# A GeGLU down projection in fp32: the order of seven-product blocks and plain K-tiles, and the step in which block sums of weights are made

## The chip, the core and the metric

The kernel runs on one core of one Trainium2 chip. A core has a matrix engine (TensorE, PE in the profile; its weight loads are listed apart as PEld), a vector engine (VectorE, DVE), a scalar engine (ScalarE, ACT), a general engine (GpSimd, POOL) and a queue engine (SyncE, SP), each with an instruction stream of its own that runs in order. They meet through semaphores. SBUF holds operands in 128 partitions, PSUM takes matmul results in eight banks of 128x512 fp32, and DMA engines move data between HBM and SBUF. The metric is the device time of one execution in microseconds (us); lower is better.

## The reference

One decoder layer on x of 256 tokens by 2048 channels, all in float32. A first half mixes tokens (eight attention heads beside sixteen state-space heads) and adds the result to x. The second half is the feed-forward part, in which the change lies:

```
h = rms_norm(x, ln_ffn_pre)
u = causal_depthwise_conv(h @ w_ffn_up, ffn_conv_w, ffn_conv_b)      # 2048 -> 2 * 5632, three taps
gate, up = jnp.split(u, [FFN_HIDDEN], axis=-1)
f = (jax.nn.gelu(gate, approximate=True) * up) @ w_ffn_down         # 5632 -> 2048
x = x + rms_norm(f, ln_ffn_post)
```

## The kernel before, in words

**Products.** A float32 product is made of three matmuls. Each operand is split into a rounded part (hi, type fp32r) and the rest (lo): hi times hi, hi times lo and lo times hi are added up in PSUM. Activations are split once. Weights are split as they arrive: a unit of weights is 128x1024 fp32 (512 KB). SP issues its load into a tile `raw` (four buffers), ACT casts it to `whi`, DVE subtracts to get `wlo` (lines 80 to 82). `whi` and `wlo` have four buffers and, from the feed-forward part on, three more, so units are prepared seven ahead of the one that PE works on. `take` hands PE the next prepared unit, `tick`, called after each unit, prepares one more. A cast into a buffer waits until PE has finished with the unit that was there.

**The feed-forward part** works in two halves of 22 hidden K-tiles (128 channels each). In each half PE first makes the up projection (`cols_tile`, lines 245 and 246) for gate and up of each K-tile; ACT and DVE do the convolution, the GELU and the product (`conv_ffn`, `gated`) and split the result. Then comes the down projection, once for output columns 0 to 1023 and once for 1024 to 2047: two calls of `down_pair` per half, four in all.

**Inside `down_pair`.** The first eight K-tiles of the half form four blocks of two K-tiles (QUADS = 4). A block is a 2x2 by 2x2 matrix product (token halves by K-tiles, K-tiles by 512 columns), made with seven products in place of eight (`product`, lines 1084 to 1086, three matmuls of 512 columns each). The seven need sums of weight blocks. So a block takes four steps of the weight stream, in `quad_step`: "col" (a loaded unit, split whole), "next" (a loaded unit, of which one half is split), "two" (a tile `ts` of two sums, split whole) and "more" (a tile `ts` of two further sums, split whole). The sums are DVE additions of 128x512 (line 137, two for each `ts`), written in the source ahead of the cast (line 138) and the subtraction (line 139) of the same step. PE does two, one, two and two products in the four steps. The other 14 K-tiles (PLAIN) go two to a unit, seven units for the first 512 columns and seven for the second, with 12 matmuls to a unit (`rows_part`, lines 309 to 311).

In each call all four blocks come first, then the 14 plain units. Four of the products' sums stand in PSUM banks `pa` (p1, p6, p7, q5), the other three go into three of the four banks `ph`, into which the plain units then add too. After the last block ACT and DVE add the four `pa` banks up in SBUF (lines 1113 to 1127); when a `ph` bank is complete, `fdone` adds it (line 1014). In the very last call the last five plain units are held and worked off token half by token half, so that the first half's norm and store run beside the second's matmuls.

**Order.** Each engine runs its stream in order. The framework that builds the streams lists instructions by their place in the source and by when it estimates that their operands are ready, so neighbours can change places: lines 1084 and 309 of a later unit stand among lines 1085 and 1086 of an earlier one in places.

**The norm weight.** Before the two down calls of the second half a POOL-issued DMA brings the post-norm weight, spread over 128 partitions (1024 KB, line 1162), into a tile `late` that reuses the memory of the up projection's input; ACT then multiplies it by -0.5 (line 1163).

Of the kernel before, what the change touches and what calls it, by code (L numbers as in the profile page):

```python
# [9 lines left out]
F32 = mybir.dt.float32  # L10
# [17 lines left out]
FF = 5632  # L28
NF = FF // P
HALF = NF // 2  # L30
QUADS = 4
PLAIN = HALF - 2 * QUADS
EPS = 1e-6
NEG = -1e30
# [22 lines left out]
def f32(ap):  # L57
    return ap.bitcast(F32)


class Weights:
# [54 lines left out]
    def quad_step(self, i, kind, src=None):  # L116

        nc, q = self.nc, self.quad  # L120
        hi, lo = (self.place(i, n, SPLB, F32R)[:, :UE] for n in ("whi", "wlo"))
        self.ready.append((hi, lo))
        n = UE
        if src is not None:
            q[kind] = raw = self.place(i, "raw", RAWB, F32)
            nc.sync.dma_start(out=raw, in_=src)
            n = UE if kind == "col" else 512
        else:
            q[kind] = raw = self.sums.tile([P, UE], F32, name="ts", tag="ts", bufs=2)
            a, b = raw[:, :512], raw[:, 512:]  # L130
            if kind == "two":
                pairs = (a, q["col"][:, 512:], q["next"][:, 512:]), (b, q["next"][:, :512],
                                                                     q["next"][:, 512:])
            else:
                pairs = (a, q["two"][:, :512], q["next"][:, :512]), (b, a, q["col"][:, :512])
            for dst, x, y in pairs:
                nc.vector.tensor_tensor(dst, x, y, op=ALU.add)  # L137
        nc.scalar.copy(hi[:, :n], raw[:, :n])  # L138
        return lambda: nc.vector.tensor_tensor(lo[:, :n], raw[:, :n], f32(hi[:, :n]),  # L139
                                               op=ALU.subtract)  # L140

# [13 lines left out]
def decoder_layer(ctx, tc, x, xT, win, wdt, wout, wup, wdown, relb, vec, cols, mconv, fconv,  # L155
# [17 lines left out]
    def psum(name):  # L173
        return msc.tile([P, 512], F32, name=name, tag="m")
# [123 lines left out]
    def col_psum():  # L298
        return acc.tile([P, 512], F32, name="pa", tag="a")
# [43 lines left out]
    def units(w, a, n, shift=0):  # L343
        return [(w[i], shift) for i in range(a, a + n)]

    def down_units(half):

        found, at = [], half * 44
        for _ in range(2):
            for j in range(QUADS):  # L350
                found += [("col", wdown[at]), ("next", wdown[at + 1]), ("two",), ("more",)]
                at += 2
            found += units(wdown, at, PLAIN)
            at += PLAIN
# [722 lines left out]
        nc.scalar.copy(hi, src)  # L1077
        nc.vector.tensor_tensor(lo, src, f32(hi), op=ALU.subtract)

    def product(ps, j, block, w, h, more=False):  # L1080

        a, b = (gx[j][:, c, :][:, tok(block)] for c in range(2))
        s = chunk(h)
        nc.tensor.matmul(ps, a, w[0][:, s], start=(j == 0), stop=False)
        nc.tensor.matmul(ps, a, w[1][:, s], start=False, stop=False)
        end[0] = nc.tensor.matmul(ps, b, w[0][:, s], start=False,
                                  stop=(j == QUADS - 1 and not more)).ins

    def down_pair(half, c):

        p1, p6, p7, q5 = (col_psum() for _ in range(4))
        pss = [[psum("ph"), psum("ph")] for _ in range(2)]
        for j in range(QUADS):
            w = ws.take()
            product(p1, j, 0, w, 1)
            product(pss[0][0], j, 1, w, 0, True)
            tick()
            w = ws.take()  # L1100
            product(pss[1][0], j, 6, w, 0, True)
            tick()
            w = ws.take()
            product(q5, j, 3, w, 0)
            product(p7, j, 5, w, 1)
            tick()
            w = ws.take()
            product(p6, j, 4, w, 0)
            product(pss[0][1], j, 2, w, 1, True)
            tick()  # L1110
        f = [[fa[:, t, chunk(c + n)] for t in range(NT)] for n in range(2)]
        tt = nc.vector.tensor_tensor
        if half == 0:
            nc.scalar.copy(f[0][0], p1)
            tt(f[1][0], p6, f[0][0], op=ALU.add)
# [3 lines left out]
        else:  # L1119
            nc.scalar.copy(e[0], p1)  # L1120
            tt(f[0][0], e[0], f[0][0], op=ALU.add)
            tt(e[0], p6, e[0], op=ALU.add)
            tt(e[1], p7, e[0], op=ALU.add)
            tt(f[0][1], e[1], f[0][1], op=ALU.add)
            for n in range(2):
                tt(f[1][n], q5, f[1][n], op=ALU.add)
                tt(f[1][n], f[1][n], e[n], op=ALU.subtract)
        n = PLAIN // 2
        for h in range(2):
            last = half == 1 and c == 2 and h == 1  # L1130
            for i in range(n - HOLD * last):
                w = ws.take()
                for t in range(NT):
                    rows_part(pss[h][t], w, gT, 2 * i, t, i == 0 and h * t == 1, i == n - 1)
                tick()
            if not last:
                for t in range(NT):
                    fdone(half, c + h)(t, pss[h][t])
        if half == 1 and c == 2:
            fearly.extend(early_sum(ss[2][t][:, :3]) for t in range(NT))  # L1140
            tail = [ws.take() for _ in range(HOLD)]
            for t in range(NT):
                for i in range(HOLD):
                    rows_part(pss[1][t], tail[i], gT, 2 * (n - HOLD + i), t, False, i == HOLD - 1)
                fdone(1, 3)(t, pss[1][t])

    defer(5, lambda: along_tokens(rb2, [sums[:, t:t + 1] for t in range(NT)]))
    for half in range(2):
        for i in range(half * HALF, (half + 1) * HALF):
            ps = held_up[2 * i:2 * i + 2]  # L1150
            for _ in range(2 - len(ps)):
                ps.append(col_psum())
                cols_tile(ps[-1], h2)
            us = [summed(p) for p in ps]
            if i < 2:
                defer(5 - 2 * i, gated, i, *us)
            else:
                gated(i, *us)
        if half == 1:
            late = pers.tile([P, D + 1024], F32, name="late", tag="h", bufs=1)  # L1160
            wpo, e = late[:, :D], [late[:, D:D + 512], late[:, D + 512:]]
            aux(out=wpo, in_=row_bcast(V_FFNPOST, D))
            nc.scalar.mul(wpo, wpo, -0.5)
        for c in (0, 2):
            down_pair(half, c)

# [104 lines left out]
```

## Time and profile before

| | |
|---|---|
| median of 3 runs | 1108.06 us (1106.46 to 1108.73) |
| the profiled execution | 1109.13 us, its span 1107.2 us |
| PE busy | 1095.1 us, 99% of the span, 5840 matmuls |
| DVE busy | 876.2 us, 79% |
| ACT busy | 617.0 us, 56% |
| DMA | 217.59 MB, mean 197 GB/s |
| mean granted TensorE clock | 0.996 of full speed |

A row of the timeline reads: start in us, duration in us, engine, line of the kernel, operation, what is written and what is read, shapes, and in brackets the idle time of the engine just before with what ended it. Matmul durations overlap (a matmul of 512 columns is listed with 0.39 us, but the next starts 0.23 us later), so time on PE is read from the distance between starts. The listing of waits gives total us, times, and the longest in us. A very few matmul records are missing.

### The profile page before, as it was taken

Reading aid. Unit: us, or ns where it says so; the run is one execution under the profiler, and the core shown is the slowest. Engines: PE = TensorE matmul, PEld = TensorE weight load, DVE = VectorE, ACT = ScalarE, POOL = GpSimd, SP = SyncE. Lnnn points to the kernel's source line nnn. Section 1 sums busy time; section 2 is a strip of 40 time slices with the busy share of each in tenths; the row PEclk is TensorE's granted clock in tenths of the full one; section 3 lists DMA queues with packets and bytes.
Section 4 is the critical chain, followed back from the end, with each engine's and each line's share of the span. In section 5 each row is a group of like instructions: output and inputs, shape, how many; then the busy total and the mean of one; then the engine's idle time right before and its main releaser. Section 6 shows DMA issues by size and latency. Waiting matters only on the chain.

```text
span 1107.2 us, 15885 instructions
## 1 busy us (share of the span) xinstructions
PE 1095.1 (99%) x5840; PEld 937.2 (85%) x5840; DVE 876.2 (79%) x1418; ACT 617.0 (56%) x938; POOL 16.2 (1%) x26
## 2 busy tenths in 40 slices
PE   9999999999999999999999999999999999999997
PEld 7888888888888988888888788888888888877886
DVE  6699976776566799888788988758788878898885
ACT  6666545545454486555555655545555555565452
POOL 0010000000000000000000000000000000000000
PEclk9999999999999999999999999999999999999999
DMA  8868545555587266666565284866556656538362
GB/s 283 303 192 269 183 152 162 180 173 170 206 305 248 86 226 226 194 190 193 189 190 188 107 274 130 286 192 191 191 190 190 191 190 190 179 127 278 132 235 78
DMA packets 61358, 217.59 MB, mean 197 GB/s; under 512 B 7200, under 2 KB 8624, under 8 KB 60384
## 3 DMA queue, kind: packets, MB, share of 16 engines
q1 hardware_dynamic: 59328, 207.64, 57.8%
q0 software_dynamic: 1664, 8.59, 2.1%
q8 instruction: 46, 0.75, 0.3%
q10 hardware_dynamic: 288, 0.35, 0.1%
q14 instruction: 32, 0.26, 0.1%
HBM read 214.44 MB, written 2.11 MB: 196 GB/s over the span
## 4 chain that ended last, share of the span: by engine, by line
PE 93%; DVE 3%; DMA 1%; ACT 1%; issue 1%; SPq 0%; POOLq 0%; ACTq 0%; DVEq 0%
PE pa L245 36%; PE pa L246 18%; PE pa L309 5%; PE pa L310 5%; PE pa L311 5%; PE ph L309 5%; PE ph L310 5%; PE ph L311 5%; DVE wlo L139 1%; PE pab L245 1%; DVE ts L137 1%; PE pa L254 1%; PE py L645 1%; PE pab L246 1%; DMA late<-in_vec_dram 1%
## 5 line engine op out<-in xcount | busy, mean ns | idle before, releaser
L81 ACT CAST whi<-raw 128x1024 fp32r<-128x1024 f32 (+2 forms) x357 | 369.7, 1039 | 337.1 <-PE pa L245 176.8
L82 DVE TENSOR_TENSOR wlo<-raw,whi 128x1024 fp32r<-128x1024 f32 (+2 forms) x357 | 429.4, 1208 | 154.1 <-ACT whi L81 147.1
L245 PE MATMUL pa<-h,whi 128*128 128x512 f32 x1360 | 471.7, 394 | 0.0
L246 PE MATMUL pa<-h,wlo 128*128 128x256 f32 x1360 | 379.1, 279 | 0.0
L245 PEld LDWEIGHTS pa<-h,whi 128*128 128x128 f32 x1360 | 255.5, 188 | 57.5
L246 PEld LDWEIGHTS pa<-h,wlo 128*128 128x128 f32 x1360 | 255.3, 188 | 0.0
L245 PE MATMUL pa<-hT,whi 128*128 128x512 f32 x384 | 137.0, 398 | 0.0
L246 PE MATMUL pa<-hT,wlo 128*128 128x256 f32 x384 | 107.1, 281 | 0.0
L309 PE MATMUL ph<-whi,gT 128*128 128x512 f32 x224 | 87.7, 392 | 0.2 <-ACT whi L81 0.2
L311 PE MATMUL ph<-whi,gT 128*128 128x512 f32 x224 | 87.4, 390 | 0.0
L310 PE MATMUL ph<-wlo,gT 128*128 128x512 f32 x224 | 87.4, 390 | 0.0
L245 PEld LDWEIGHTS pa<-hT,whi 128*128 128x128 f32 x384 | 72.5, 189 | 15.5 <-issue 0.2
L1005 DVE SCALAR_TENSOR_TENSOR cfc<-cfu,fcv,cfc 128x255 f32<-128x255 f32 (+1 forms) x176 | 83.1, 477 | 1.6 <-ACT cfc L1003 0.4
L246 PEld LDWEIGHTS pa<-hT,wlo 128*128 128x128 f32 x384 | 72.3, 189 | 0.4 <-issue 0.2
L1003 ACT ACTIVATE cfc<-cfu,fcv 128x256 f32<-128x256 f32 x88 | 52.2, 598 | 1.1 <-DVE cfu L1002 1.1
L138 ACT CAST whi<-ts 128x1024 fp32r<-128x1024 f32 x32 | 33.5, 1048 | 33.8 <-DVE ts L137 14.4
L309 PE MATMUL pa<-whi,hT 128*128 128x512 f32 x128 | 51.1, 400 | 0.0
L309 PEld LDWEIGHTS ph<-whi,gT 128*128 128x128 f32 x224 | 42.3, 189 | 9.5 <-ACT whi L81 0.7
L309 PE MATMUL pa<-whi,mT 128*128 128x512 f32 x128 | 50.3, 393 | 0.0
L311 PE MATMUL pa<-whi,hT 128*128 128x512 f32 x128 | 50.1, 392 | 0.0
L310 PE MATMUL pa<-wlo,hT 128*128 128x512 f32 x128 | 50.0, 390 | 0.0
L310 PE MATMUL pa<-wlo,mT 128*128 128x512 f32 x128 | 50.0, 390 | 0.0
(257 smaller groups left out, 1340.2 us busy)
## 6 DMA issues: line engine op xcount, KB each, us to landing
raw<-in_wup_dram SPq DMA_DIRECT2D x176, 512.0 KB, 3.6
raw<-in_wdown_dram SPq DMA_DIRECT2D x88, 512.0 KB, 4.3
raw<-in_win_dram SPq DMA_DIRECT2D x85, 512.0 KB, 3.6
raw<-in_wout_dram SPq DMA_DIRECT2D x32, 512.0 KB, 4.1
xsq<-in_x_dram SPq DMA_DIRECT2D x2, 1024.0 KB, 9.2
rows<-acd POOLq DMA_DIRECT2D x4, 512.0 KB, 6.7
xt<-in_x_dram POOLq DMA_DIRECT2D x2, 1024.0 KB, 6.8
xr<-in_xT_dram SPq DMA_DIRECT2D x6, 256.0 KB, 6.8
```

The lines of the kernel that those rows point to most:

```text
L81: nc.scalar.copy(hi[:, s], raw[:, s])
L82: return lambda: nc.vector.tensor_tensor(lo[:, s], raw[:, s], f32(hi[:, s]), op=ALU.subtract)
L137: nc.vector.tensor_tensor(dst, x, y, op=ALU.add)
L138: nc.scalar.copy(hi[:, :n], raw[:, :n])
L139: return lambda: nc.vector.tensor_tensor(lo[:, :n], raw[:, :n], f32(hi[:, :n]), op=ALU.subtract)
L245: nc.tensor.matmul(ps, w[0][:, s], both, start=(k == 0), stop=False)
L246: end[0] = nc.tensor.matmul(ps[:, c], w[1][:, s], hi, start=False, stop=(k == KT - 1)).ins
L309: nc.tensor.matmul(ps, a, w[0][:, s], start=(first and j == 0), stop=False)
L310: nc.tensor.matmul(ps, a, w[1][:, s], start=False, stop=False)
L311: end[0] = nc.tensor.matmul(ps, b, w[0][:, s], start=False, stop=(last and j == 1)).ins
L1003: nc.scalar.activation(c, u, AF.Identity, scale=wv[:, 2:3], bias=wv[:, 3:4])
L1005: nc.vector.scalar_tensor_tensor(c[:, sh:], u[:, :S - sh], wv[:, 2 - sh:3 - sh], c[:, sh:], op0=ALU.mult, op1=ALU.add)
```

## The change

Four edits. First, the order inside `down_pair` is now a string, ORDER, read once per call: Q is a block with its four steps, 0 and 1 are plain units for the first and the second 512 columns. There are still four blocks and seven plain units for each 512 columns, and the last five entries are the ones held in the very last call. The list of weight units and the host's array follow the same string, in `down_units` and in the host code.

Second, the steps of a block are now "same" (split whole), "other" (one half split), "two" and "more". The sums of "two" are made in step "other", with one addition of 128x1024 whose second operand repeats a half unit twice; the sums of "more" are made in step "two", with two additions of 128x512. The two loaded units hold other pairs of blocks than before, so that this works.

Third, the multiplication of the post-norm weight by -0.5 is issued not ahead of the second half's down calls but in the first of them, behind its fourth block.

Fourth, the additions of the four `pa` banks move into `quad_sums`, which is called behind the fourth block, so ahead of the plain units that follow it. `fdone` for the first 512 columns is called behind the seventh unit 0.

```
+ORDER = "0Q01Q001Q0Q0011111"
+QUADS = ORDER.count("Q")
...
+        else:
+            raw = q[kind]
+        if kind == "other":
+            n = 512
         nc.scalar.copy(hi[:, :n], raw[:, :n])
+        if kind == "other":
+            q["two"] = to = self.sums.tile([P, UE], F32, name="ts", tag="ts", bufs=2)
+            two = (ap.rearrange("p (b c) -> p b c", b=2) for ap in (to, q["same"]))
+            add(*two, raw[:, None, 512:].to_broadcast([P, 2, 512]), op=ALU.add)
+        elif kind == "two":
+            q["more"] = to = self.sums.tile([P, UE], F32, name="ts", tag="ts", bufs=2)
+            add(to[:, :512], raw[:, :512], q["same"][:, 512:], op=ALU.add)
+            add(to[:, 512:], to[:, :512], q["other"][:, :512], op=ALU.add)
         return lambda: nc.vector.tensor_tensor(lo[:, :n], raw[:, :n], f32(hi[:, :n]),
                                                op=ALU.subtract)
...
+        for what in ORDER[:-HOLD] if last else ORDER:
+            if what == "Q":
+                for items in (((p1, 0, 0), (pss[1][0], 6, 1)), ((pss[0][0], 1, 0),),
+                              ((q5, 3, 0), (p7, 5, 1)), ((p6, 4, 0), (pss[0][1], 2, 1))):
+                    multiply(items, ws.take())
+                    tick()
+            else:
+                w, h, i = ws.take(), int(what), done[what]
                 for t in range(NT):
+                    rows_part(pss[h][t], w, gT, 2 * i, t, first(pss[h][t]), i == n - 1)
                 tick()
+            done[what] += 1
+            if what == "Q" and done[what] == QUADS:
+                if half == 1 and c == 0:
+                    nc.scalar.mul(wpo, wpo, -0.5)
+                quad_sums(half, c, *once)
+            elif what != "Q" and done[what] == n:
                 for t in range(NT):
                     fdone(half, c + h)(t, pss[h][t])
...
             aux(out=wpo, in_=row_bcast(V_FFNPOST, D))
-            nc.scalar.mul(wpo, wpo, -0.5)
```

More of the change, by code (lines that the diff above doesn't have):

```diff
@@ L116, in quad_step @@
     def quad_step(self, i, kind, src=None):
-        nc, q = self.nc, self.quad
+        nc, q, add = self.nc, self.quad, self.nc.vector.tensor_tensor
         hi, lo = (self.place(i, n, SPLB, F32R)[:, :UE] for n in ("whi", "wlo"))
@@ L348, in down_units @@
         found, at = [], half * 44
-        for _ in range(2):
-            for j in range(QUADS):
-                found += [("col", wdown[at]), ("next", wdown[at + 1]), ("two",), ("more",)]
+        for what in 2 * ORDER:
+            if what == "Q":
+                found += [("same", wdown[at]), ("other", wdown[at + 1]), ("two",), ("more",)]
                 at += 2
-            found += units(wdown, at, PLAIN)
-            at += PLAIN
+            else:
+                found += units(wdown, at, 1)
+                at += 1
         return found
@@ L1078, in quad_operands, with product, quad_sums @@
         nc.vector.tensor_tensor(lo, src, f32(hi), op=ALU.subtract)
-    def product(ps, j, block, w, h, more=False):
+    def product(ps, j, block, w, h, first, last):
         a, b = (gx[j][:, c, :][:, tok(block)] for c in range(2))
         s = chunk(h)
-        nc.tensor.matmul(ps, a, w[0][:, s], start=(j == 0), stop=False)
+        nc.tensor.matmul(ps, a, w[0][:, s], start=first, stop=False)
         nc.tensor.matmul(ps, a, w[1][:, s], start=False, stop=False)
[L1086 to L1110, printed above, removed]
+        end[0] = nc.tensor.matmul(ps, b, w[0][:, s], start=False, stop=last).ins
+    def quad_sums(half, c, p1, p6, p7, q5):
         f = [[fa[:, t, chunk(c + n)] for t in range(NT)] for n in range(2)]
@@ L1118, in down_pair @@
             tt(f[1][0], q5, f[1][0], op=ALU.subtract)
[L1119 to L1132, printed above, removed]
+            return
@@ new lines, in quad_sums, with down_pair, first, multiply @@
+        nc.scalar.copy(e[0], p1)
+        tt(f[0][0], e[0], f[0][0], op=ALU.add)
+        tt(e[0], p6, e[0], op=ALU.add)
+        tt(e[1], p7, e[0], op=ALU.add)
+        tt(f[0][1], e[1], f[0][1], op=ALU.add)
+        for n in range(2):
+            tt(f[1][n], q5, f[1][n], op=ALU.add)
+            tt(f[1][n], f[1][n], e[n], op=ALU.subtract)
+    def down_pair(half, c):
+        once = [col_psum() for _ in range(4)]
+        p1, p6, p7, q5 = once
+        pss = [[psum("ph"), psum("ph")] for _ in range(2)]
+        begun, done, n = set(), {"Q": 0, "0": 0, "1": 0}, PLAIN // 2
+        def first(ps):
+            new = id(ps) not in begun
+            begun.add(id(ps))
+            return new
+        def multiply(items, w):
+            for ps, block, h in items:
+                product(ps, done["Q"], block, w, h, first(ps),
+                        done["Q"] == QUADS - 1 and any(ps is z for z in once))
+        last = half == 1 and c == 2
+        for what in ORDER[:-HOLD] if last else ORDER:
+            if what == "Q":
+                for items in (((p1, 0, 0), (pss[1][0], 6, 1)), ((pss[0][0], 1, 0),),
[4 more added lines that the diff above has]
+                w, h, i = ws.take(), int(what), done[what]
@@ L1137, in down_pair @@
                 for t in range(NT):
                     fdone(half, c + h)(t, pss[h][t])
-        if half == 1 and c == 2:
+        if last:
             fearly.extend(early_sum(ss[2][t][:, :3]) for t in range(NT))
```

31 lines of the change are left out of this document (13 added, 18 removed).

## The prediction

> **What bounds the kernel now.** I began with the page's first part and its chain of waits.
>
> ```profile
> PE 1095.1 (99%) x5840; PEld 937.2 (85%) x5840; DVE 876.2 (79%) x1418; ACT 617.0 (56%) x938; POOL 16.2 (1%) x26
> PE 93%; DVE 3%; DMA 1%; ACT 1%; issue 1%; SPq 0%; POOLq 0%; ACTq 0%; DVEq 0%
> ```
>
> PE carries the time. The change takes no matmul away: four blocks of 21 matmuls and 14 plain units of 12 make 4 x 21 + 14 x 12 = 252 per down call, before and after. So it can only win what PE loses inside the four down calls. Next come the starts of PE's instructions at the calls' borders, from the timeline.
>
> ```profile
> 616.36 0.39 PE L1084 MATMUL pa<-whi,gx 128*128 128x512 f32 x1
> ...
> 637.33 0.39 PE L309 MATMUL ph<-whi,gT 128*128 128x512 f32 x1
> ...
> 675.41 0.39 PE L1084 MATMUL pa<-whi,gx 128*128 128x512 f32 x1
> ...
> 732.95 0.40 PE L245 MATMUL pa<-h,whi 128*128 128x512 f32 x1
> ...
> 977.01 0.39 PE L1084 MATMUL pa<-whi,gx 128*128 128x512 f32 x1
> ...
> 1040.22 0.39 PE L1084 MATMUL pa<-whi,gx 128*128 128x512 f32 x1
> ...
> 1097.60 1.25 PE L1029 MATMUL pa<-xt,cst 128*128 128x256 f32 x6
> ```
>
> The 168 plain matmuls of the first call run from 637.33 to 675.41: 0.2267 us each, so a call without a pause is 252 x 0.2267 = 57.12 us. The four calls take 59.05 (616.36 to 675.41), 57.54, 63.21 and 57.38 us. PE loses 1.93 + 0.42 + 6.09 + 0.26 = 8.70 us there: that is all there is to win. The rest after 1097.60 is the last norm and store, which keeps its five held units. The pauses themselves, first call and third:
>
> ```profile
> 633.60 0.73 PE L1084 MATMUL pa<-whi,gx 128*128 128x512 f32 x2 [0.51 <-ACT whi L138]
> 634.92 0.50 PE L1084 MATMUL pa<-whi,gx 128*128 128x512 f32 x1 [0.59 <-ACT whi L138]
> ...
> 989.61 0.50 PE L1085 MATMUL pa<-wlo,gx 128*128 128x512 f32 x1 [0.62 <-DVE wlo L139]
> ...
> 998.45 0.50 PE L1084 MATMUL pa<-whi,gx 128*128 128x512 f32 x1 [2.27 <-ACT whi L138]
> ...
> 999.73 0.74 PE L1085 MATMUL pa<-wlo,gx 128*128 128x512 f32 x1
> 1000.27 0.63 PE L1086 MATMUL pa<-whi,gx 128*128 128x512 f32 x1
> ...
> 1003.23 0.40 PE L310 MATMUL ph<-wlo,gT 128*128 128x512 f32 x1
> ```
>
> All lie near the end of the four blocks, and PE waits for the split of block weights. Behind the 2.27 us pause eight starts take 1003.23 - 999.73 = 3.50 us where 1.81 were due: PE ran at about half clock, which makes 1.69 of the 6.09 us.
>
> Why the splits are late is read on DVE, inside the first call:
>
> ```profile
> 629.38 1.82 DVE L139 TENSOR_TENSOR wlo<-raw,whi 128x1024 fp32r<-128x1024 f32 x2
> 631.12 1.29 DVE L137 TENSOR_TENSOR ts<-raw 128x512 f32<-128x512 f32 x2
> 632.32 1.41 DVE L137 TENSOR_TENSOR ts<-ts,raw 128x512 f32<-128x512 f32 x2
> 633.65 2.48 DVE L139 TENSOR_TENSOR wlo<-ts,whi 128x1024 fp32r<-128x1024 f32 x2
> 636.04 4.62 DVE L82 TENSOR_TENSOR wlo<-raw,whi 128x1024 fp32r<-128x1024 f32 x4
> 640.59 0.68 DVE L1115 TENSOR_TENSOR fa<-pa,fa 128x512 f32<-128x512 f32 x1
> ```
>
> One block costs DVE 636.04 - 629.38 = 6.66 us without a gap, and PE only 21 x 0.2267 = 4.76. A plain unit costs DVE 4.55 / 4 = 1.14 us and PE 12 x 0.2267 = 2.72. Four blocks in a row put DVE 4 x 1.90 = 7.6 us behind; the prepared lead pays for most of it, and PE stands for the rest. Over a whole call DVE needs 4 x 6.66 + 14 x 1.14 = 42.6 us of 57.12: the average fits, the order doesn't.
>
> The third call has an extra cause, seen on ACT, in the chain of waits and in SP's waits:
>
> ```profile
> 983.94 1.92 ACT L1163 ACTIVATE late<-late 128x2048 f32<-128x2048 f32 x1 [1.81 <-DMA late<-in_vec_dram]
> 985.76 0.39 ACT L232 CAST gT<-cfc 128x256 fp32r<-128x256 f32 x1
> ```
> ```profile
> 989.47 0.70 DVE ts L137
> 990.18 4.12 DMA raw<-in_wdown_dram
> 994.40 1.06 ACT whi L81
> ```
> ```profile
> SPq L80 <- DVE ts L137: 17.2, 4, 10.2
> ```
>
> ACT stands 1.81 us for the norm weight's DMA and then works 1.92 us on it, with casts and the last K-tile's products queued behind. The block sums come late, they keep the `raw` buffers, the next load starts only at 990.18 and lands 4.12 us later, and PE stands at 996. The third call loses 6.09 - 1.93 = 4.16 us more than the first, whose blocks stand in the same order.
>
> **The interleaved order.** I count PE time from a call's start. The order gives 0 at 0, first block 2.72, two units, second block at 2.72 + 4.76 + 5.44 = 12.92, three units, third block 25.8, one unit, fourth block 33.3, done by 38.1. How much is prepared at the start is shown by ACT:
>
> ```profile
> 613.67 0.62 ACT L138 CAST whi<-raw 128x512 fp32r<-128x512 f32 x1 [1.45 <-PE pa L245]
> ...
> 616.44 1.05 ACT L138 CAST whi<-ts 128x1024 fp32r<-128x1024 f32 x1 [1.84 <-PE pa L245]
> ```
>
> These are steps six and seven of the weight stream (second block's "next" and "two"): at 616.4 seven steps are there or in work. In the old order seven steps hold 4.76 us and most of a second block, some 8 us of PE. In the new they are 0, block, 0, 1: 12.9 us. In that time DVE owes the second block, 6.66, and the rest of the last K-tile's convolution, eight instructions between and with these two:
>
> ```profile
> 618.66 0.42 DVE L263 TENSOR_TENSOR cfu<-pa,cfu 128x256 f32<-128x256 f32 x1
> ...
> 624.72 0.41 DVE L233 TENSOR_TENSOR gT<-cfc,gT 128x256 fp32r<-128x256 f32 x1
> ```
>
> At some 0.45 each that is 3.6 us, together 10.3 of the 12.9. A cast waits until PE is done seven steps back. The tightest is then the fourth block's "two": free when PE finishes the third block's "same", at 27.2, needed at 33.3 + 3 x 0.68 = 35.4; 8 us for a cast of 1.05 and a subtraction of 1.22. The third block falls due 12.9 us behind the second and the fourth 7.5 behind the third, against 6.66 + 3 x 1.14 = 10.1 and 7.8 of DVE time; the 0.3 come out of that lead. So the DVE pauses go: up to 1.93 + 0.42 + 0.26, and 1.93 of the third call's. What is late next is nothing on PE's inputs; its own 57.12 us is.
>
> A rule of the Trainium skill bears on the half-clock stretch, in "TensorE: Matmul & The Clock Gate", Part 1: the clock falls back only after an idle window of about 3.4 us. Here it fell with a longest idle row of 2.27 us. By this rule of the Trainium skill the 1.69 us would not belong to this pause and would stay, and the sum would be 1102.1. The trace has them right behind the pause, so I count them with it.
>
> **The sums one step ahead.** Line 137 runs ahead of earlier splits already:
>
> ```profile
> 958.84 0.69 DVE L137 TENSOR_TENSOR ts<-raw 128x512 f32<-128x512 f32 x1 [0.17 <-DMA raw<-in_wdown_dram]
> 959.45 1.22 DVE L82 TENSOR_TENSOR wlo<-raw,whi 128x1024 fp32r<-128x1024 f32 x1
> ```
>
> So I give this edit zero of its own, beyond letting `raw` go a step sooner. It turns two additions of 0.60 (starts of line 137) into one of 1024 columns with a repeated operand, which no row shows; the nearest is 1.14 for 1024 columns. Between 0.06 us gained and, if the repeat doubled it, 1.1 lost per block, it lies beside PE: DVE has 57.12 - 42.6 = 14.5 us a call, less 4.2 for seven additions of `pa` and 4.8 for `fdone` (eight of 0.60), 5.5 left; four times 1.1 still fits. I take 0.06, off the path. The new addition needs its loaded unit, and DVE's queue (subtractions, evacuations) stands behind it; PE's seven-step lead covers that (priced below).
>
> **The norm weight.** ACT's 3.73 us (1.81 and 1.92) leaves the start of the third call. Its 1.92 goes to about 38 us into the call, where five plain units lie prepared or free. The DMA stays at the start and shares the engines with weight loads, of which the next seven are in. This brings the 4.16 us. If the lead were gone, it would cost 1.92 once.
>
> **The sums of `pa`, earlier.** Five to eight instructions of 0.60 at 38 us, with seven plain units (19 us of PE) left, on DVE that is 1.14 of 2.72 busy there. In the last call the first 512 columns' `fdone` comes at 43.5; its 4 x 0.6 us ends well before the first token half's 30 held matmuls (6.8 us). No term.
>
> **Sum.** 8.70 us out of the profiled execution's 1109.13 gives 1100.4. I keep 0.2 for stray pauses: 1100.6. The profiled execution lies 1.07 us above the median of the runs, 1108.06, which gives 1099.5. Between the two: 1100.0 us. A difference of 0.2%, 2.2 us, is about what a measurement here can tell from none.
>
> **Rivals.** *Half the gain.* The norm weight's DMA (1024 KB) still delays the third call's loads, or the start's convolution work still does, so that 4.16 us stay: 1104.2. For it: the DMA stays where it is. Against: seven steps are in by then.
>
> *No change.* The streams are listed by estimated readiness, so the list could draw blocks together again, or another wait (loads: ACT's row below) could take the pauses' place: 1108.1. Against: a unit goes to PE in the order of the list.
>
> *Slower: DVE's head of line.* The 1024-column addition waits for "other" to land, and everything queued on DVE waits with it.
>
> ```profile
> ACT whi L81 <- DMA raw<-in_wdown_dram: 19.9, 19, 2.5
> ```
>
> That row of the second half's down calls gives 1.05 us per wait for a load. If each of 16 blocks paid it on PE, 16.8 - 8.7 = 8.1 us slower: 1116.2. It decides from (8.7 + 2.2) / 16 = 0.68 us per block that nothing covers. Against: waits of that kind lie mostly in the plain stretch now, where PE has no pause.
>
> *Slower: the clock.* PE changes between seven PSUM banks and two, eight times a call. If each of 32 changes set off one half-clock stretch of 1.69 us, 54 us: 1154 after the gain. Against it, a change that exists, and the clock while banks change every three matmuls (in a row by stretches, the 1.00 behind the five engines' busy times):
>
> ```profile
> 628.00:631.00 3.00, 3.00 (x14) 2.29 (x13) 2.96 (x4) 1.68 (x3) 0.00 (x0) 1.00 0.78 307
> ```
> ```profile
> 675.18 0.39 PE L311 MATMUL ph<-whi,gT 128*128 128x512 f32 x1
> 675.41 0.39 PE L1084 MATMUL pa<-whi,gx 128*128 128x512 f32 x1
> ```
>
> At 675.41 the change from plain units to a block costs nothing. The Trainium skill has it as a rule, in "TensorE: Matmul & The Clock Gate", section "A second HAM failure mode: psum-queue depth-cycling": cycling through PSUM banks makes PE idle briefly between groups, often enough that the clock swings. This trace does not agree.
>
> **Chances.** Forecast 0.77, half the gain 0.13, no change 0.05, head of line 0.04, clock 0.01. Faster 0.77 + 0.13 = 0.90, same 0.05, slower 0.05. The range runs from 1098.0 (all 8.70 off 1106.46, the fastest run, is 1097.8) to 1104.2, the half gain; what is left out is the other 0.10 and what noise adds.
>
> **What would show it.** Down calls of 57.1 to 57.6 us, all four; no row of PE waiting for line 138's or 139's successors; clock 1.00 in the third; ACT without a wait for `late`; block additions of 1024 columns near 1.2 us; the time behind the last down matmul as before (9.6 us of span). Wrong: a call above 58.5, a new PE wait at a block's first matmul, or the 8.70 us back in the up projection.

## The result and the profile after

The changed kernel took 1100.97 us (median of four runs, 1100.4 to 1101.27) beside 1108.39 for the kernel before in the same session (1106.46 to 1110.66). The ratio is 0.9932, with a 95% interval of 0.9912 to 0.9951: 7.4 us won, and between 5.4 and 9.8 by the interval. The profiled executions stand at 1100.73 and 1109.13 us, 8.40 apart. The ratios given below leave out one execution of the run with less for DVE, which took 1827.68 us at a granted clock of 0.556.

The page of the changed kernel, busy times and the chain that ended last:

```profile
PE 1089.9 (99%) x5840; PEld 936.4 (85%) x5840; DVE 873.1 (79%) x1402; ACT 617.5 (56%) x938; POOL 16.2 (1%) x26
PE 94%; DVE 3%; DMA 1%; issue 1%; ACT 1%; POOLq 0%; ACTq 0%; DVEq 0%
```

The matmuls are as many as before, and DVE has 16 instructions fewer: two additions of 512 columns became one of 1024 in each of 16 blocks. The timeline of PE at the calls' borders, and at the one place where it stands in them:

```profile
615.47 0.39 PE L312 MATMUL ph<-whi,gT 128*128 128x512 f32 x1
...
672.62 0.39 PE L312 MATMUL ph<-whi,gT 128*128 128x512 f32 x1
...
729.74 0.40 PE L248 MATMUL pa<-h,whi 128*128 128x512 f32 x1
...
973.80 0.39 PE L312 MATMUL ph<-whi,gT 128*128 128x512 f32 x1
...
1030.95 0.39 PE L312 MATMUL ph<-whi,gT 128*128 128x512 f32 x1
...
1034.12 0.39 PE L1090 MATMUL pa<-whi,gx 128*128 128x512 f32 x1
1035.15 0.50 PE L1088 MATMUL ph<-whi,gx 128*128 128x512 f32 x1 [0.64 <-DVE fa L1018]
...
1089.03 1.25 PE L1033 MATMUL pa<-xt,cst 128*128 128x256 f32 x6
```

The down calls take 57.15, 57.12, 57.15 and 58.08 us, against 59.05, 57.54, 63.21 and 57.38 before. The floor is 57.12, so three calls have nothing left to lose and the fourth has 0.96. Together that is 229.50 in place of 237.18: 7.68 won, of 8.70 that there were. The span went down by 8.6: the other 0.9 lies ahead of the first down matmul (615.47 for 616.36), in code that the change leaves alone; 0.6 of it is there by the first row `pa<-whi,hT`, at 52.23 us for 52.83. In the profiles of the other runs below, in either order, the first down matmul stands between 615.59 and 616.19, so this part varies by itself. The up projection of the second half takes 244.06 us in both. So the gain of the edit is the 7.68.

All that PE waits for, by the listing of waits (total us, times, longest):

```profile
PE pa L1039 <- ACT diag L1037: 2.7, 1, 2.7
PE idle L380 <- DVE junk L377: 1.1, 1, 1.1
PE ph L1088 <- DVE fa L1018: 0.6, 1, 0.6
```

The first two stood in the listing before, at the final norm and in the first half of the layer. The lines that were the split of block weights (3.4 and 0.6 us) are gone. What is new is the third. DVE in the stretch where the first call of before fell behind, by stretches (us, then busy time of PE, PEld, DVE, ACT and POOL, clock, DMA share, GB/s), changed kernel first:

```profile
613.00:640.00 27.00, 27.00 (x125) 22.46 (x124) 22.60 (x30) 16.23 (x20) 0.00 (x0) 1.00 0.57 175
```
```profile
613.00:640.00 27.00, 25.89 (x117) 20.72 (x116) 25.92 (x38) 16.64 (x22) 0.00 (x0) 1.00 0.38 133
```

DVE was busy 25.92 of 27 us there and is busy 22.60 now, for eight matmuls more. The work is the same over a call; it no longer falls due in one lump.

The row that the prediction watched for the norm weight, ACT at the start of the third call:

```profile
979.07 1.04 ACT L133 CAST whi<-ts 128x1024 fp32r<-128x1024 f32 x1
982.17 1.92 ACT L1146 ACTIVATE late<-late 128x2048 f32<-128x2048 f32 x1 [2.05 <-DMA late<-in_vec_dram]
983.99 1.02 ACT L133 CAST whi<-ts 128x1024 fp32r<-128x1024 f32 x1
```

In the source the multiplication stands behind the fourth block. In ACT's stream it stands near the call's start, 8.4 us behind the first matmul (6.9 before), with a wait of 2.05 us ahead of it. The time came all the same, so the prediction's reason for the largest of its terms needed testing.

### The profile page after: what moved, and what is told of

It reads as the page before. It is cut to its first block, busy times and chain, and to the rows that moved or that the text cites. A ratio compares the mean times of both kernels' runs of the same rounds, so it can differ in the third digit from the quotient of the medians.

```text
span 1098.6 us, 15877 instructions
## 1 busy us (share of the span) xinstructions
PE 1089.9 (99%) x5840; PEld 936.4 (85%) x5840; DVE 873.1 (79%) x1402; ACT 617.5 (56%) x938; POOL 16.2 (1%) x26
## 4 chain that ended last, share of the span: by engine, by line
PE 94%; DVE 3%; DMA 1%; issue 1%; ACT 1%; POOLq 0%; ACTq 0%; DVEq 0%
PE pa L248 37%; PE pa L249 19%; PE pa L312 5%; PE pa L314 5%; PE pa L313 5%; PE ph L314 3%; PE ph L312 3%; PE ph L313 3%; DMA raw<-in_wdown_dram 1%; PE pab L248 1%; PE pa L1090 1%; PE pa L1088 1%; PE pa L1089 1%; PE ph L1088 1%; PE ph L1090 1%
## 5 line engine op out<-in xcount | busy, mean ns | idle before, releaser
L312 PE MATMUL pa<-whi,mT 128*128 128x512 f32 x128 | 50.3, 393 | 0.0
L314 PE MATMUL pa<-whi,mT 128*128 128x512 f32 x128 | 49.9, 390 | 0.0
```

Of the source, the lines that this page charges most:

```text
L312: nc.tensor.matmul(ps, a, w[0][:, s], start=(first and j == 0), stop=False)
L314: end[0] = nc.tensor.matmul(ps, b, w[0][:, s], start=False, stop=(last and j == 1)).ins
```

## The experiments

**The theory** at this point: blocks that follow each other put DVE behind, and that is what PE pays for. **Rivals:** ACT's stand for the norm weight makes the third call's extra loss (the prediction's own step), or the sums made a step ahead make the gain. Lengths below are of both down calls of a half, from the first down matmul to the next stage; the floor for the two is 114.26 us (504 matmuls). Before they were 116.59 and 120.59, after 114.27 and 115.23.

### The multiplication moved alone

In the kernel before:

```
-            nc.scalar.mul(wpo, wpo, -0.5)
...
+        if half == 1 and c == 0:
+            nc.scalar.mul(wpo, wpo, -0.5)
```

(The added lines stand in `down_pair`, behind the fourth block.)

> The kernel before, with only the multiplication of the norm weight moved behind the fourth block of the third down call. My theory: the third call loses what the first does, so its 63.21 us become about 59.1, the half-clock stretch goes with the long pause, and the run is 4.2 us faster than before. Rival A (ACT's stand for the norm weight is only the last of several causes; the loads kept back by the block sums are the real one): the third call stays above 61 us and the gain is under 2 us. Rival B (the norm weight is the whole cause of the gain): 7 us faster or more.

Measured: 116.60 and 121.41 us, median 1108.64, ratio 1.0003 (0.9994 to 1.0012). ACT's row:

```profile
984.51 1.92 ACT L1112 ACTIVATE late<-late 128x2048 f32<-128x2048 f32 x1 [2.98 <-DMA late<-in_vec_dram]
```

The line number is the new one; the place in ACT's stream is the old, between the same two neighbours as before. So this run can't say what the stand is worth; it shows that moving a line in the source didn't move the instruction. ACT happened to wait 1.17 us longer here (2.98 for 1.81), and the third call took 64.05 us in place of 63.21.

### The change with the multiplication left where it was

In the changed kernel the two added lines go and the multiplication returns to its place behind the DMA.

```
-                if half == 1 and c == 0:
-                    nc.scalar.mul(wpo, wpo, -0.5)
...
+            nc.scalar.mul(wpo, wpo, -0.5)
```

> The changed kernel, with the multiplication of the norm weight back at the start of the third down call. As my prediction summed them, the two edits add: the third call would then lose some 4 us and the run would take about 1105. Rival (the new order's lead of about 12.9 us of PE work covers ACT's 3.7 us): the third call stays within 1 us of 57.1, and the time is that of the changed kernel, about 1101.

Measured: 114.27 and 118.35 us, median 1100.52, ratio 0.9936 (0.9924 to 0.9949). The median is the full gain, so the third edit is worth nothing that these runs can tell. The profiled execution was this kernel's slowest, 1104.26 (the other four 1100.17 to 1100.64), and shows where it lost:

```profile
1034.43 0.39 PE L1090 MATMUL pa<-whi,gx 128*128 128x512 f32 x1
1037.10 0.80 PE L1088 MATMUL ph<-whi,gx 128*128 128x512 f32 x1 [2.27 <-DVE fa L1018]
1037.69 0.63 PE L1089 MATMUL ph<-wlo,gx 128*128 128x512 f32 x1
1038.12 0.63 PE L1090 MATMUL ph<-whi,gx 128*128 128x512 f32 x1
```

The third call is free of pauses although ACT waits 2.63 us for the norm weight in it. All the loss is at the fourth call's first block, the place where the changed kernel lost 0.96, here 4.1 with the half-clock starts (0.43 us apart) behind the pause.

### The change with the blocks in a row

```
-ORDER = "0Q01Q001Q0Q0011111"
+ORDER = "QQQQ00000001111111"
```

> The changed kernel with the four blocks first again and then the fourteen plain units; the sums one step ahead and the late multiplication stay. My theory: DVE falls 1.9 us behind per block again, first and third call lose about 1.9 us each, second and fourth some 0.3 each; gain over before 4 to 4.5 us, about 1104.3. Rival (making the sums a step ahead is what matters, since PE waited for their split): calls of 57.5 or less and a time of about 1101. A second rival (the sums ahead hold DVE up): slower than before in those calls, above 1106.

Measured: 117.16 and 119.48 us, median 1108.07, ratio 0.9999 (0.9990 to 1.0008). Nothing is left of the gain; 1104.3, as expected by the theory, was too low. In the profile the third call is 1.2 us shorter than before (62.00) and without half clock, the first 0.6 longer (59.62). The pauses are those of before, at the end of the blocks:

```profile
995.59 0.73 PE L1088 MATMUL pa<-whi,gx 128*128 128x512 f32 x2 [1.23 <-ACT whi L133]
997.17 0.50 PE L1089 MATMUL pa<-wlo,gx 128*128 128x512 f32 x1 [0.84 <-DVE wlo L142]
```

The three other edits, without the interleaved order, make no difference that can be measured.

### The sums in their own step

The interleaved order stays, the sums move back behind the loads, ahead of the cast that needs them:

```
-            raw = q[kind]
+            q[kind] = raw = self.sums.tile([P, UE], F32, name="ts", tag="ts", bufs=2)
+            if kind == "two":
+                two = (ap.rearrange("p (b c) -> p b c", b=2) for ap in (raw, q["same"]))
+                add(*two, q["other"][:, None, 512:].to_broadcast([P, 2, 512]), op=ALU.add)
+            else:
+                add(raw[:, :512], q["two"][:, :512], q["same"][:, 512:], op=ALU.add)
+                add(raw[:, 512:], raw[:, :512], q["other"][:, :512], op=ALU.add)
```

> The changed kernel, interleaved, but each block's sums are made in the step that splits them, ahead of its cast, as before. My theory: no term of its own, the time of the changed kernel (1100.5 to 1101.5), all four calls within 1 us of 57.1. Rival (the sums ahead are needed, since a cast that waits for its sums keeps later casts behind it on ACT): pauses of 0.5 us or more at blocks, 2 us or more slower than the changed kernel.

Measured: 114.27 and 116.19 us, median 1100.98, ratio 0.9937 (0.9925 to 0.9949). The same as the change. Of the 1.93 us lost in the second half's profile, 1.5 are again at the fourth call's first block, with an idle row of 1.20; most of the rest is at 1081.7 us. The profiled execution was this kernel's slowest, 1103.29 (the other four 1099.81 to 1101.19).

### ACT without the multiplication, blocks in a row

The factor goes into the instruction that uses the weight, in the kernel before. Then nothing on ACT waits for the weight's DMA.

```
-            nc.scalar.mul(wpo, wpo, -0.5)
...
-                nc.vector.tensor_tensor(f, f, wpo[:, chunk(c)], op=ALU.mult)
+                nc.vector.scalar_tensor_tensor(f, f, -0.5, wpo[:, chunk(c)], op0=ALU.mult, op1=ALU.mult)
```

> The kernel before without the multiplication of the norm weight on ACT; the factor -0.5 goes into the DVE product with that weight, which is one instruction before and after. In the run where only its place in the source was moved, ACT's row for it stayed at the start of the third call. My theory of the prediction: the third call loses 4.2 us by ACT's stand, so it comes down to about 59.1 us and the time to about 1104.2. Rival (the loads held back by the block sums make the third call long, and the norm weight's 1024 KB load makes it worse whoever reads it): the third call stays above 61 us, gain under 2 us.

Measured: 116.59 and 119.85 us, median 1107.17, ratio 0.9984 (0.9975 to 0.9993). The third call goes from 63.21 to 62.49, not to the 59 of the first call. ACT's stand is worth 0.72 us in the profile, and 0.8 to 2.8 us by the interval of the ratio; the prediction had it at 4.16. PE still stands at the end of the blocks, and the half clock still follows:

```profile
997.36 0.50 PE L1084 MATMUL pa<-whi,gx 128*128 128x512 f32 x1 [2.50 <-ACT whi L138]
```

What ACT's last block cast (line 138) waits for is on DVE, and DVE's own rows show what stands there:

```profile
996.26 1.04 ACT L138 CAST whi<-ts 128x1024 fp32r<-128x1024 f32 x1 [1.42 <-DVE ts L137]
```
```profile
992.24 1.22 DVE L139 TENSOR_TENSOR wlo<-ts,whi 128x1024 fp32r<-128x1024 f32 x1
993.38 0.68 DVE L137 TENSOR_TENSOR ts<-ts,raw 128x512 f32<-128x512 f32 x1
994.40 1.23 DVE L82 TENSOR_TENSOR wlo<-raw,whi 128x1024 fp32r<-128x1024 f32 x1 [0.34 <-ACT whi L81]
995.54 0.69 DVE L137 TENSOR_TENSOR ts<-ts,raw 128x512 f32<-128x512 f32 x1
```

Between the two additions (line 137) of the last `ts` stands the split of a plain unit (line 82), which PE needs only later: 0.34 us of waiting for ACT and 1.14 of work, just ahead of the sum that PE stands for. The split of `ts` at 992.24 stands ahead of it too. In the first call the last sums stand ahead of both splits of `ts`, and of every plain split:

```profile
631.84 1.41 DVE L137 TENSOR_TENSOR ts<-ts,raw 128x512 f32<-128x512 f32 x2
633.17 2.47 DVE L139 TENSOR_TENSOR wlo<-ts,whi 128x1024 fp32r<-128x1024 f32 x2
```

For the first 9.3 us DVE's rows in the two calls agree to 0.02 us. Then they are listed in another order, and the last sum ends 17.4 us into the first call and 19.7 us into the third. That made a new suspect, the order of the list.

### The same removal in the changed kernel

The edit is the one above, in the changed kernel, where the two lines behind the fourth block go.

> The changed kernel without that multiplication on ACT, in the same way. The changed kernel has one PE pause left, about 0.8 us at the start of the fourth call, where the first product into a bank waits for DVE to add up the third call's result. If that lateness is what ACT's stand in the third call left behind: the pause goes, all calls 57.1 to 57.3, 0.5 to 1.5 us faster than the changed kernel. Rival (it is only the order in which DVE's stream lists that addition behind splits): the pause stays, same time as the changed kernel.

Measured: 114.26 and 114.27 us, median 1100.65, ratio 0.9930 (0.9917 to 0.9942). All four calls at the floor. The fourth call's pause is gone, and the median is 0.3 us below that of the change, which these runs can't tell from nothing. In the profile 0.6 of the 0.96 us are lost again at the end, 10.21 us behind the last down matmul in place of 9.57. DVE at that place, changed kernel and then this one:

```profile
1032.14 1.23 DVE L142 TENSOR_TENSOR wlo<-ts,whi 128x1024 fp32r<-128x1024 f32 x1 [1.17 <-ACT whi L133]
1033.28 1.22 DVE L83 TENSOR_TENSOR wlo<-raw,whi 128x1024 fp32r<-128x1024 f32 x1
1034.41 1.28 DVE L1018 TENSOR_TENSOR fa<-ph,fa 128x512 f32<-128x512 f32 x2
```
```profile
1029.78 1.23 DVE L142 TENSOR_TENSOR wlo<-ts,whi 128x1024 fp32r<-128x1024 f32 x1 [1.17 <-ACT whi L133]
1030.92 1.22 DVE L83 TENSOR_TENSOR wlo<-raw,whi 128x1024 fp32r<-128x1024 f32 x1
1032.06 1.28 DVE L1018 TENSOR_TENSOR fa<-ph,fa 128x512 f32<-128x512 f32 x2
```

The list is the same: the addition that empties the `ph` banks of the third call (line 1018) stands behind two splits, the first of which waits 1.17 us for its cast. A product of the fourth call's first block waits for that bank. Without ACT's stand all of it comes 3.0 us earlier, counted from the fourth call's start (1030.95 and 1031.57), and that is enough.

### One more unit ahead of the first block

```
-ORDER = "0Q01Q001Q0Q0011111"
+ORDER = "00Q01Q01Q0Q0011111"
```

> The changed kernel with the order 00Q01Q01Q0Q0011111: two plain units ahead of the first block, two between second and third. If the pause of the fourth call is the first block's product waiting for its bank, 2.7 us more cover end it: all calls 57.1 to 57.3 and 0.5 to 1.5 us faster than the changed kernel. If the tighter spacing behind (blocks two to four with 10.2 and 7.5 us between their starts against 6.66 us of DVE work each and the units') matters: pauses at blocks three and four of 0.5 us or more, same time or slower than the changed kernel.

Measured: 114.26 and 114.27 us, median 1100.56, ratio 0.9929 (0.9917 to 0.9942). The pause is gone here too, with ACT's stand in place: the order alone can cover it.

### The new addition made twice

```
-            two = (ap.rearrange("p (b c) -> p b c", b=2) for ap in (to, q["same"]))
+            two = list(ap.rearrange("p (b c) -> p b c", b=2) for ap in (to, q["same"]))
+            add(*two, raw[:, None, 512:].to_broadcast([P, 2, 512]), op=ALU.add)
```

> The changed kernel with the 1024-column addition of each block issued twice, the second time with the same result: 1.14 us more DVE work per block, 4.6 us per call. My prediction's bound says that DVE has 5.5 us left in a call, so this stays beside PE: within 1 us of the changed kernel. Rival (DVE's order, not its sum, is at its limit): pauses at blocks, above 1103.

Measured: 114.27 and 116.42 us, median 1102.54, ratio 0.9946 (0.9933 to 0.9958). In the first half the 1.14 us more per block cost nothing. In the second the fourth call loses 2.15 us, against 0.96 in the change, and now mostly at its second block:

```profile
1048.79 0.51 PE L1089 MATMUL pa<-whi,gx 128*128 128x512 f32 x1 [0.25 <-ACT whi L133]
1050.05 0.50 PE L1090 MATMUL pa<-wlo,gx 128*128 128x512 f32 x1 [0.75 <-DVE wlo L143]
```

### Blocks in a row, with the list mended

The kernel of the run without the multiplication, and in it the casts and splits of the three plain units behind a block are listed after that block's last cast and split:

```
+        if not any(self.units[z][0] == "more" for z in range(i - 3, i)):
+            return self.rounded(*self.tiles(i), slice(0, UE))
+        with self.tc.issue_after(self.cast):
+            sub = self.rounded(*self.tiles(i), slice(0, UE))
+
+        def behind():
+            with self.tc.issue_after(self.sub):
+                sub()
+        return behind
...
```

(Behind the cut, `quad_step` keeps its cast and its subtraction as `self.cast` and `self.sub`.)

> The kernel before without the norm weight's multiplication on ACT, and with one thing more: the casts and subtractions of the three plain units behind a fourth block are listed behind those of the block's last step. In the run without this, the third call still lost 5.3 us: a plain unit's cast stood on ACT, waiting for PE's buffer, ahead of the last block's casts, and its subtraction stood on DVE ahead of the last sums. Theory now: that place in the list is the third call's extra loss; with it mended the pause of 2.5 us and the half-clock stretch go, third call about 59, time 1103.5 to 1105. Rival (DVE's backlog alone makes the third call's loss, and the list only shows it): third call stays above 61, time as without it, about 1107.

Measured: 116.19 and 119.04 us, median 1105.67, ratio 0.9969 (0.9957 to 0.9981). The third call takes 61.67 us, 0.82 less than without this edit: what it moves is a part, and a small one. DVE in the third call, without a gap:

```profile
994.50 0.68 DVE L145 TENSOR_TENSOR ts<-ts,raw 128x512 f32<-128x512 f32 x1
995.10 1.27 DVE L1138 TENSOR_TENSOR fa<-pa,fa 128x512 f32<-128x512 f32 x2
996.35 1.23 DVE L149 TENSOR_TENSOR wlo<-ts,whi 128x1024 fp32r<-128x1024 f32 x1
997.49 4.69 DVE L82 TENSOR_TENSOR wlo<-raw,whi 128x1024 fp32r<-128x1024 f32 x4
```

The plain units' splits (line 82) now stand behind the last block split (line 149), and the last sum ends 18.7 us into the call in place of 19.7. But two bank additions (line 1138), 1.25 us, stand ahead of that split, as two did without the edit (lines 1121 and 1126, 996.15 to 997.35 us in that run), and a split of `ts` still stands ahead of the last sum. So the edit undid only a part of what sets the third call's list apart from the first's.

### Blocks in a row, with less for DVE

In the kernel before, with the multiplication on ACT and the list as it was, the two additions of each block's last step are made 32 columns wide instead of 512, and the step splits the sums of the step before. So this kernel leaves out two of the sums that the seven products need; only its time is of use. The edit:

```
+                raw = q["two"]
+                few = self.sums.tile([P, 64], F32, name="few", tag="few", bufs=2)
+                a, b = few[:, :32], few[:, 32:]
-                pairs = (a, q["two"][:, :512], q["next"][:, :512]), (b, a, q["col"][:, :512])
+                pairs = (a, raw[:, :32], q["next"][:, :32]), (b, a, q["col"][:, :32])
```

> The kernel before, blocks first, leaving out the sums of each block's last step: that step splits the sums of the step before once more, and two additions of 32 columns keep the loaded buffers as long as before. DVE's work for a block falls by about 1.0 us, 4 us in a call. If DVE's backlog of 1.9 us per block is what PE stands for in the first two calls, their losses of 1.9 and 0.4 us fall to under 0.5 together. The third call should lose 2 us less too, to about 61. Rival (loads kept back by the held buffers, not DVE, are late): first call stays above 58.5.

Measured: 114.27 and 116.18 us, median 1101.59, ratio 0.9935 (0.9921 to 0.9948). DVE is busy 860.2 us in place of 876.2: 1.0 us less for each of 16 blocks. That alone gives nearly the whole gain, with blocks in a row and ACT's stand in place. The third call takes 59.06 us, 4.15 less than before; its pauses are these, with no half clock behind them:

```profile
990.86 0.50 PE L1087 MATMUL pa<-whi,gx 128*128 128x512 f32 x1 [0.31 <-ACT whi L141]
992.38 0.50 PE L1088 MATMUL pa<-wlo,gx 128*128 128x512 f32 x1 [1.02 <-DVE wlo L142]
992.72 0.39 PE L1089 MATMUL pa<-whi,gx 128*128 128x512 f32 x1
```

So the third call's loss, too, hung on DVE's backlog. The edit also lets the last step's cast go without new sums. That this by itself isn't the gain is shown by the change with the blocks in a row, where the sums are made a step ahead and the ratio is 0.9999.

### Five blocks

Once DVE has room, a block can replace two plain units (21 matmuls for 24). From the changed kernel without the multiplication:

```
-ORDER = "0Q01Q001Q0Q0011111"
+ORDER = "0Q01Q0Q0Q0Q011111"
...
-        u = fp.tile([P, S], F32, name="cfu", tag="cf", bufs=8)
+        u = fp.tile([P, S], F32, name="cfu", tag="cf", bufs=6)
...
-        c = fp.tile([P, S], F32, name="cfc", tag="cf", bufs=8)
+        c = fp.tile([P, S], F32, name="cfc", tag="cf", bufs=6)
```

> The changed kernel without the multiplication on ACT, with five blocks and twelve plain units in the order 0Q01Q0Q0Q0Q011111, and six in place of eight convolution buffers to make room. PE work per call falls by three matmuls, 0.68 us, 2.7 us in all: 1097.9 if DVE keeps up. DVE then has 5 x 6.66 + 12 x 1.14 = 47.0 us of splits and sums in a call, and 56 of 56.4 with the second half's additions; the run with the sums made twice lost 2.2 us in the second half at 56 of 57. Theory: first half down calls without loss, second half loses 2 to 5 us: 1099 to 1103. Rival (the lead covers it): below 1098.5.

Measured: 112.91 and 113.21 us, median 1099.38, ratio 0.9913 (0.9900 to 0.9927). The floor is 112.90 (498 matmuls), so the calls are all but free of pauses: the 2 to 5 us that the theory saw lost in the second half came to 0.31, and the time lies in its range only because the end grew. It has the lowest median of all kernels here, 1.3 us below the same kernel with four blocks (1100.65); the intervals of the two ratios overlap. The two halves are 2.41 us shorter than with four blocks. Of these, 1.04 went at the end, which takes 11.25 us behind the last down matmul (1086.35 to the span's 1097.6) where it took 10.21 with four blocks. Why is seen on DVE:

```profile
1084.72 2.74 DVE L1044 SCALAR_TENSOR_TENSOR xt<-fa,lsr,xt 128x512 f32<-128x512 f32 x4
...
1086.35 1.25 PE L1033 MATMUL pa<-xt,cst 128*128 128x256 f32 x6
1087.38 0.69 DVE L1018 TENSOR_TENSOR fa<-ph,fa 128x512 f32<-128x512 f32 x1
```

The first token half's norm (line 1044) runs on DVE until 1087.4, and the second token half's last bank addition (line 1018), whose matmuls are over about when PE goes on at 1086.35, stands behind it. PE's wait at the final norm is 3.80 us there, and 2.70 with four blocks.

### Five blocks, placed earlier

```
-ORDER = "0Q01Q001Q0Q0011111"
+ORDER = "0Q0Q1Q0Q0Q0011111"
```

The other edits are those of the run above.

> As the run with five blocks, but in the order 0Q0Q1Q0Q0Q0011111: one plain unit between blocks throughout and two behind the last block. In the run before, the down calls took 226.1 us, and the end of the program behind the last down matmul 11.25 us in place of 9.57: DVE came late to the last norm, because the bank additions fell next to it. If that is so, the end goes back to 9.6 us with one unit more behind the last block, and the time is about 1.5 us below that run's 1099.4: 1097.5 to 1098.3. Rival (DVE is at its limit in the second half, 56 of 56.4 us a call, and what it wins at the end comes back as pauses at blocks): the second half's down calls lose 1 to 3 us, 1099 or more.

Measured: 112.90 and 114.42 us, median 1099.56, ratio 0.9917 (0.9903 to 0.9930). The end takes 10.57 us, 0.68 less, but the last call has a pause for a block split again (extra 1.22 us). Nothing is won over the run above: as the rival had it, what DVE wins at the end comes back as a pause at a block.

## Why the prediction was right, and which step of it failed

The forecast was 1100.0 us, between 1098.0 and 1104.2; the median is 1100.97.

**What there was to win** was right: 8.70 us of pauses in the four calls, of which 7.68 went. The profiled execution took 1100.73 us, and the sum said 1100.6. This agreement is partly luck: the sum lacked 0.96 us lost in the fourth call, and had no term for the 0.9 us that the part ahead of the down calls was shorter in this execution.

**DVE's backlog of 1.9 us a block as the cause** was right, and shown from two sides: the old order in the changed kernel takes the gain away (0.9999), and 1.0 us less DVE work a block in the old order brings it (0.9935).

**The sums one step ahead, zero** was right: with the sums in their own step the ratio is 0.9937 beside the change's 0.9932. The price of the new addition, which no row of before showed, was put at 1.14 to 1.2 us. By operation and tile (first row: duration in ns, lowest, median and highest):

```profile
L137 DVE TENSOR_TENSOR ts<-raw x16: 1214/1218/1226, 599.3 to 1056.7; 128x1024 f32<-128x1024 f32 x16
...
  DMA raw<-in_wdown_dram: 7.0, 5
```

The repeated operand costs nothing. The head of line that the slower rival feared is the second row: DVE stood 7.0 us, five times, ahead of this addition for a load. PE paid for none of it, as the prediction had it: the listing of what PE waits for has no split of a weight left in it.

**"This brings the 4.16 us"** is the step that failed, the one on the norm weight. Moving the line didn't move the instruction; ACT still waits 2.05 us for the DMA. Its stand was worth 0.72 us in the profile, not 4.16, where it could be taken away with the blocks in a row (ratio 0.9984, about 1.5 us in the median). DVE's rows show how little of it arrives: with the stand, DVE waits 0.73 us for ACT's cast of `gT`, and its last sum ends 20.3 us into the third call in place of 19.7. The 4.16 us came back through the first edit: with the multiplication at the call's start, the interleaved third call takes 57.15 us.

The third call of before loses 6.09 us, and 5.37 without the stand, where the first call loses 1.9. What the rows show to set the two calls apart by then is the order of DVE's list, with the last sum 2.3 us later, and the half clock behind the longest pause. Moving the plain units' splits took 0.82 us off. With a lighter DVE, and the list and ACT's stand as they were, only 1.94 of the 6.09 remain (59.06 for a floor of 57.12). The rows quoted for ACT were there, but with the multiplication gone the pause ahead of the last block's cast was 2.50 us, longer than the 2.27 that they had been made to explain. What went wrong was to take the difference between two calls in which one visible cause differs for the price of that cause. In the second half there is also more on DVE: it adds the banks with eight instructions where the first half has four, and two or three of them stand ahead of the last split of the third call.

**"What is late next is nothing"** failed by 0.96 us. At the border of the third and fourth call a bank's addition stands on DVE behind two splits. It is the head-of-line mechanism of the slower rival, at one place in place of 16, and for a bank and not for a load. Its size varied in the profiles of near kernels (a pause of 0.64 us in the change, 1.20 and 2.27 in two others of that order), and one unit more ahead of the first block removes it.

**"Four times 1.1 still fits"** was right in the first half and wrong in the second: with the addition made twice 2.15 us are lost there, and 0.96 with it made once. The average over a call has the room; the place where it falls due had not. That is the mistake that the prediction had named for the order before, made again for the new one.

**The clock** was right: 1.00 in the third call's former slow stretch, where it was 0.68.

```profile
1000.00:1005.00 5.00, 5.00 (x24) 4.14 (x23) 5.00 (x7) 2.36 (x3) 0.00 (x0) 1.00 0.47 150
```

The 1.69 us of half clock went with the pause ahead of them, as the prediction counted them; the sum of 1102.1 us, in which they stay, did not come. **The end** was right too: 9.57 us behind the last down matmul, 9.6 before. In the other runs with four interleaved blocks it is 9.6 to 10.9, so part of this agreement is luck.

**What stays open.** The interval of the ratio doesn't tell the change from its variants between 0.9929 and 0.9937. In the third call, what each difference of the list is worth was not tried one by one, nor the half clock apart from its pause. The norm weight's DMA (1024 KB) starts with that call in every run and was never moved, so its own share isn't known. Differences between two profiles, such as 0.72 and 0.82 us, are no sharper than about 0.8: the third call took 63.21 us in the kernel before and 64.05 with the line moved, though ACT's row stood at the same place. What sets the size of the fourth call's pause from one execution to the next was not tried.

## What to carry to other kernels

Where one engine prepares what another uses, compare their times for each kind of step and not only over the stage, and mix the steps that leave the preparer behind with those that let it catch up, before single instructions are moved or removed. After a line has been moved in the source, look for its row in the trace: a framework that lists by readiness may have put it back. A difference between two stages is the price of a cause only when a run has taken that cause away.

## What the runs showed of the hardware

Half clock (starts 0.43 us apart in place of 0.23, for seven to nine matmuls) followed pauses with a longest idle row of 2.27 us in the kernel before, 2.27, 2.40 and 2.50 in others, and 1.59 (with one of 0.22 behind it) in the run with the mended list. It didn't follow idle rows of 1.23 and 0.84 us two matmuls apart (the change with the blocks in a row), of 1.02, or of 1.20. The kernel before, by stretches around the fall (us, then busy time of PE, PEld, DVE, ACT and POOL, clock, DMA share, GB/s):

```profile
996.37:999.78 3.41, 1.12 (x4) 0.56 (x4) 3.41 (x6) 2.43 (x3) 0.00 (x0) 1.00 0.89 288
999.78:1003.19 3.41, 3.41 (x9) 2.71 (x9) 2.37 (x3) 1.65 (x3) 0.00 (x0) 0.50 0.73 263
1003.19:1006.60 3.41, 3.41 (x16) 2.78 (x15) 3.41 (x5) 2.01 (x2) 0.00 (x0) 1.00 0.92 297
```

In all five runs with such a stretch in a down call, it lasts 3.41 us at clock 0.50. In every run the changes of the clock lie whole multiples of 3.413 us apart: here the fall comes 993.28 us, 291 of them, behind the first rise. So the length of a pause alone doesn't decide. On that grid the clock fell behind stretches in which PE was busy 1.60 us or less, and kept full speed behind those of 1.92 or more; behind one of 1.57 it kept it too, so the limit is known only roughly. The final norm shows how much the place on the grid counts. Behind the same wait of 2.70 us, six matmuls took 1.35 us in the changed kernel and 2.50 in the one without the multiplication on ACT. The Trainium skill, in "TensorE: Matmul & The Clock Gate", Part 1, names an idle window of about 3.4 us; in these runs less was enough, and the runs decide.

PE changed between two and seven PSUM banks 32 times in the changed kernel, with three of the four calls at the 0.2267 us a matmul of plain units.
